# Expert blocks of a two-layer MoE kernel: 184 blocks in 46 groups become 176 blocks in 44 groups, in another order

## The chip, the cores and the metric

The kernel runs on one core of a Trainium2 chip, as one launch. The metric is the device time of that launch in microseconds (us); a kernel's time is the median of its runs. TensorE is called PE here (its matmuls; its weight loads are PEld), VectorE DVE, ScalarE ACT, GpSimd POOL, and SP is the engine whose queue issues most DMAs.

## The reference

Two layers over 2048 tokens of 1024 features. Layer 0 mixes the tokens with latent attention, layer 1 with pooled means; each is followed by a layer norm, a mixture of experts and a second layer norm. Both experts parts are alike:

```
g_sel  = argmax(h @ w_grp + b_grp)                 # one of 8 groups
top_p, top_i = top_k(softmax(e_logits of that group), 2)
expert = g_sel * 8 + top_i                         # 2 of 64 experts for each token
gate   = g_gate * top_p / sum(top_p)
y      = (silu(x @ w1[e]) * (x @ w3[e])) @ w2[e]   # d_expert = 256
out[token] += y * gate
```

So 4096 choices (2048 tokens, two each) are spread over 64 experts in each layer, unevenly, and every expert's 3 MB of weights (w1, w3 and w2, 1 MB each, float32) are needed once in each layer.

## The kernel before

The router (Router, lines 457 to 638) counts, token tile by token tile, how many tokens chose each expert. Once 14 of the 16 tiles are counted it sorts the experts by that count. An expert's position in this sort is its *place*: place 0 is the expert with the most tokens. Places 13 to 16 are an exception: they hold four experts of the middle, chosen after nine tiles, so that their weights can be fetched early. What a place means is fixed when the program is written; which expert stands at it is data.

Work is cut into blocks of 32 slots (QS). A block (p, q) holds the tokens number 32q to 32q+31 of the expert at place p. Four blocks make a group of 128 rows (function groups). Each place has a fixed number of blocks, by AT4, AT3 and AT2: 6 for places 0 to 2, 4 for places 3 to 12, 3 for places 13 to 36, and 2 for places 37 to 63. That is 184 blocks in 46 groups. Tokens that find no slot are done by overflow(), a loop whose number of turns is counted on the chip by counts(); it is entered with zero turns if every expert fits.

WORK is the order of the groups, and LINE the order in which their places come up first. Moe.main runs one step for each group in WORK. Step i gathers 128 token rows for step i+3 (an indirect DMA on POOL's queue), multiplies group i with w1 and w3 (up, line 1313: 64 matmuls that read up to four experts' weights), multiplies the group of step i-1 with w2 (down, line 1341: 32 matmuls) and scatters its rows to memory, then transposes the rows of a later group (line 1301) and the activations of group i (line 1326). PE executes this in program order.

load_line (line 1277) writes the weight loads into SP's queue in the order of LINE: for each place w13 (two DMAs of 1 MB, line 1249) and w2 (one, line 1254). There are five w13 and five w2 buffers in layer 0, six and six in layer 1; place number n of LINE reuses the buffer of number n-5 or n-6, once the last group that reads that one is done (ENDS). SP is in order: a load that waits for its buffer holds up those behind it. The first three places' weights (nine DMAs) are loaded before the experts begin. The DMA semaphores are eight that go round, so a load is issued when the eighth one before it has landed.

Behind layer 1's last group, ending() and rest() fetch what the last norm reads (w<-ln_g, w<-ln_b, ten w<-X, six fx<-X; lines 973, 974, 1608, 1616) into weight buffers that have come free. After overflow's loop last_norm reads Y.

Router.finish (line 625) makes the tables of source rows, target rows and gates for all groups, with one pair of small matmuls for each run that block_runs finds; counts() makes each place's limit lim (lines 1425, 1426).

Of the kernel before, what the change touches and what calls it, by code (L numbers as in the profile page):

```python
# [25 lines left out]
NE = 64  # L26
HP = P // 2
QS = 32
NQ = P // QS
RANKS = 192  # L30

AT4, AT3, AT2 = 3, 13, 37
NPRE = 4
FIRST_ORDER_AT = 8
ORDER_AT = 13
# [34 lines left out]
def groups():  # L70

    sixes = [[(p, q) for q in range(4)] for p in range(AT4)]
    fours = [[(p, q) for q in range(4)] for p in range(AT4, AT3)]
    rests = [[(p, 4), (p, 5), (AT2 + p, 0), (AT2 + p, 1)] for p in range(AT4)]
    line = [(p, q) for p in range(AT3, AT2) for q in range(3)]
    threes = [line[i:i + NQ] for i in range(0, len(line), NQ)]
    line = [(p, q) for p in range(AT2 + AT4, NE) for q in range(2)]
    twos = [line[i:i + NQ] for i in range(0, len(line), NQ)]
    every = sixes + fours + rests + threes + twos
    n = [0]  # L80
    for x in (sixes, fours, rests, threes, twos):
        n.append(n[-1] + len(x))
    big = [[g] for g in range(n[1], n[2])] + [[g, n[2] + g] for g in range(n[1])]
    mid = [[g, g + 1, g + 2] for g in range(n[3], n[4], 3)]
    small = [[g] for g in range(n[4], n[5])]
    work = mid.pop(0)
    for i in range(len(big)):
        for part in (small, big, mid if i % 3 == 1 else []):
            if part:
                work = work + part.pop(0)  # L90
    work += [g for part in (mid, small) for x in part for g in x]
    assert sorted(work) == list(range(len(every)))
    return every, work


GROUPS, WORK = groups()
G = len(GROUPS)

# [4 lines left out]
def block_runs():  # L103

    def steps(x):
        return slice(x[0], x[-1] + 1, x[1] - x[0] if len(x) > 1 else 1)

    found = {}
    for g, blocks in enumerate(GROUPS):
        for j, (p, q) in enumerate(blocks):  # L110
            kind = next(i for i, end in enumerate((AT3, AT2, AT2 + AT4, NE)) if p < end)
            found.setdefault((kind, j, q), []).append((p, g))
    out = []
    for (_, j, q), run in found.items():
        ps, gs = [p for p, _ in run], [g for _, g in run]
        for x in (ps, gs):
            assert len({b - a for a, b in zip(x, x[1:])}) <= 1, x
        out.append((j, q, steps(ps), steps(gs)))
    return out
# [347 lines left out]
class Router:  # L467
# [157 lines left out]
    def finish(self, pool, tag):  # L625
        nc, c, w = self.nc, self.c, self.work
        flat = w.tile([P, RANKS], F32, name="ohp", bufs=2)
        nc.vector.tensor_copy(flat, self.ptab)
        pf = self.psum.tile([P, 2, G], F32, name="plog")
        for j, q, places, gs in block_runs():  # L630
            nc.tensor.matmul(pf[j * QS:(j + 1) * QS, :, gs], flat[:, q * QS:(q + 1) * QS], self.perm[:, :, places],
                             start=True, stop=True, tile_position=(0, j * QS))
        val = w.tile([P, 2, G], F32, name="fval", bufs=1)
        nc.vector.tensor_copy(val, pf)
        self.isrc, self.idst = slot_rows(nc, w, pool, val[:, 0, :], G, tag)
        self.gate = pool.tile([P, G], F32, name=f"gate{tag}")
        nc.vector.tensor_copy(self.gate, val[:, 1, :])
# [582 lines left out]
class Moe:  # L1220
# [180 lines left out]
    def counts(self):  # L1401

        nc, c, r, pool = self.nc, self.c, self.r, self.pool

        def col(name, n=1):
            return pool.tile([NE, n], F32, name=name, bufs=1)

        pc = self.psum.tile([P, 2, F], F32, name="ph", bufs=2)
        nc.tensor.matmul(pc[:NE, 0, 0:1], r.ohsum, c.onesb[:, 0:1], start=True, stop=True)
        own = col("cown", 2)  # L1410
        nc.vector.tensor_copy(own[:, 0:1], pc[:NE, 0, 0:1])
        nc.vector.tensor_copy(own[:, 1:2], c.tok1[:NE, 0:1])
        yield

        pc = self.psum.tile([P, 2, F], F32, name="ph", bufs=2)
        nc.tensor.matmul(pc[:NE, 0, 0:2], r.perm[:NE, 0, :], own, start=True, stop=True)
        cnt = col("cnt", 2)
        nc.vector.tensor_copy(cnt, pc[:NE, 0, 0:2])
        yield

        lim = col("lim")
        nc.vector.memset(lim, -6.0 * QS)
        step = col("limstep")
        for start, n in ((AT4, 2), (AT3, 1), (AT2, 1)):
            nc.vector.tensor_scalar(step, c.tok1[:NE, 0:1], start + 0.5, float(n * QS), op0=ALU.is_gt, op1=ALU.mult)
            nc.vector.tensor_tensor(lim, lim, step, op=ALU.add)
        nc.vector.tensor_scalar(lim, lim, -1.0, None, op0=ALU.mult)
        thr = col("thr", S // P)
        nc.vector.tensor_scalar(thr, c.iota[:NE, 0:S // P], float(P), lim, op0=ALU.mult, op1=ALU.add)
        cmp = col("cmp", S // P)  # L1430
        nc.vector.tensor_scalar(cmp, thr, cnt[:, 0:1], None, op0=ALU.is_lt)
        ov = col("ov1")
        nc.vector.tensor_reduce(ov, cmp, axis=AX.X, op=ALU.add)
        pcum = self.psum.tile([P, 2, F], F32, name="ph", bufs=2)
        nc.tensor.matmul(pcum[:NE, 0, 0:1], c.triinc[:NE, :NE], ov, start=True, stop=True)
        yield
        cum = col("cum", 2)
        nc.vector.tensor_copy(cum[:, 1:2], pcum[:NE, 0, 0:1])
        nc.vector.tensor_tensor(cum[:, 0:1], cum[:, 1:2], ov, op=ALU.subtract)
        member, after = col("member", NE), col("after", NE)  # L1440
        nc.vector.tensor_scalar(member, c.iota[:NE, 0:NE], cum[:, 0:1], None, op0=ALU.is_ge)
        nc.vector.tensor_scalar(after, c.iota[:NE, 0:NE], cum[:, 1:2], None, op0=ALU.is_ge)
        nc.vector.tensor_tensor(member, member, after, op=ALU.subtract)
        yield
        first = col("first")
        nc.vector.tensor_scalar(first, cum[:, 0:1], float(-P), lim, op0=ALU.mult, op1=ALU.add)
        vals = col("vals", 2 * NE)
        nc.vector.tensor_scalar(vals[:, 0:NE], member, cnt[:, 1:2], None, op0=ALU.mult)
        nc.vector.tensor_scalar(after, member, float(FAR), float(-FAR), op0=ALU.mult, op1=ALU.add)
        nc.vector.tensor_scalar(vals[:, NE:], member, first, None, op0=ALU.mult)  # L1450
        yield
        pb = self.psum.tile([P, 2, F], F32, name="ph", bufs=2)
        nc.tensor.matmul(pb[:, 0, 0:2 * NE], c.ones[:NE, :], vals, start=True, stop=True)
        nc.tensor.matmul(pb[:, 0, 2 * NE:3 * NE], c.ones[:NE, :], member, start=True, stop=True)
        nc.tensor.matmul(pb[:, 0, 3 * NE:3 * NE + 1], c.ones[:NE, :], ov, start=True, stop=True)
        self.bl = pool.tile([P, 2, NE], F32, name="bl", bufs=1)
        bl = self.bl
        valid = pool.tile([P, NE], F32, name="valid", bufs=1)
        nc.vector.tensor_copy(valid, pb[:, 0, 2 * NE:3 * NE])
        nc.vector.tensor_tensor(bl[:, 0, :], pb[:, 0, 0:NE], valid, op=ALU.subtract)  # L1460

        nc.vector.tensor_scalar(bl[:, 1, :], valid, float(-FAR), float(FAR), op0=ALU.mult, op1=ALU.add)
        nc.vector.tensor_tensor(bl[:, 1, :], bl[:, 1, :], pb[:, 0, NE:2 * NE], op=ALU.add)
        nc.vector.scalar_tensor_tensor(bl[:, 1, :], c.iota[:, 0:NE], float(P), bl[:, 1, :], op0=ALU.mult, op1=ALU.add)
        self.total = pool.tile([1, 1], I32, name="total", bufs=1)
        nc.vector.tensor_copy(self.total, pb[0:1, 0, 3 * NE:3 * NE + 1])
        self.jt = pool.tile([P, 1], F32, name="jt", bufs=1)
        nc.vector.memset(self.jt, 0.0)
# [196 lines left out]
```

## Time and profile before

| | us |
|---|---|
| median of 3 runs | 3085.59 |
| the runs | 3077.85 to 3090.36 |
| the profiled execution | 3076.86 |
| its span | 3075.2 |
| layer 0's groups: first up to end of the last down | 1524.8 to 2111.9 |
| layer 1's groups: first up to end of the last down | 2402.8 to 2975.1 |

Times in the trace are counted from the span's start. The two stretches of experts are 1159 us of the 3075. In the rows below "w<-in_w_dram" is a weight load, "ph" the result of up, "py" of down, "xg<-X,isrc" the gather and "Y<-y,idst" the scatter. Such a row of the order of time gives start, duration, engine, line and operation, how many instructions were merged, and in brackets how long the engine had been idle before it and what ended that.

### The profile page before, as it was taken

Reading aid. Unit: us, or ns where it says so; the run is one execution under the profiler, and the core shown is the slowest. Engines: PE = TensorE matmul, PEld = TensorE weight load, DVE = VectorE, ACT = ScalarE, POOL = GpSimd, SP = SyncE. Lnnn points to the kernel's source line nnn. Section 1 sums busy time; section 2 is a strip of 40 time slices with the busy share of each in tenths; the row PEclk is TensorE's granted clock in tenths of the full one; section 3 lists DMA queues with packets and bytes.
Section 4 is the critical chain, followed back from the end, with each engine's and each line's share of the span. In section 5 each row is a group of like instructions: output and inputs, shape, how many; then the busy total and the mean of one; then the engine's idle time right before and its main releaser. Section 6 shows DMA issues by size and latency. Waiting matters only on the chain.

```text
span 3075.2 us, 50829 instructions
## 1 busy us (share of the span) xinstructions
PE 2697.8 (88%) x19378; PEld 1507.0 (49%) x19378; DVE 1516.2 (49%) x3756; ACT 864.3 (28%) x1465; POOL 972.0 (32%) x838
## 2 busy tenths in 40 slices
PE   6987888888888888999799999897888799999977
PEld 5864554445454454688533333333777333333323
DVE  7655677677676776445521111223998221111118
ACT  4444343334343334323211111112454111111102
POOL 4244455455454544321211111112542111111100
PEclk9997999999999999999899999998898899999988
DMA  6544122121221211545699999995424899999967
GB/s 209 184 147 157 46 70 70 56 77 53 70 66 50 77 32 50 156 150 186 235 368 418 412 415 399 374 418 208 176 92 193 320 419 417 415 410 411 416 264 293
DMA packets 230242, 690.22 MB, mean 224 GB/s; under 512 B 42318, under 2 KB 102990, under 8 KB 180588
## 3 DMA queue, kind: packets, MB, share of 16 engines
q1 hardware_dynamic: 191484, 586.01, 50.2%
q0 software_dynamic: 27104, 69.90, 5.9%
q10 hardware_dynamic: 11408, 31.02, 2.6%
q8 instruction: 155, 2.54, 0.3%
q14 instruction: 91, 0.75, 0.1%
HBM read 595.47 MB, written 120.71 MB: 233 GB/s over the span
## 4 chain that ended last, share of the span: by engine, by line
PE 30%; DMA 20%; DVE 6%; issue 2%; POOL 1%; SPq 0%; ACT 0%; DVEq 0%; POOLq 0%; ACTq 0%; another core or an unknown queue 0%
DMA w<-in_w_dram 16%; PE ph L1313 12%; PE py L1341 5%; PE pz L1050 5%; PE pt L1301 2%; PE plog L501 2%; PE fz L1529 1%; DVE ohp L568 1%; DMA pw<-in_pool_w_dram 1%; DMA xg<-X,isrc 1%; PE rpt L992 1%; DVE goh L512 0%; DMA fy<-Y 0%; PE pz L1193 0%; PE ptab L572 0%
## 5 line engine op out<-in xcount | busy, mean ns | idle before, releaser
L1313 PE MATMUL ph<-w,xT 128*32 128x512 f32 x5888 | 682.4, 603 | 38.9 <-DMA w<-in_w_dram 38.8
L1313 PEld LDWEIGHTS ph<-w,xT 128*32 128x32 f32 x5888 | 199.5, 111 | 448.8 <-issue 430.2
L879 POOL TENSOR_TENSOR acc<-acc,pe 128x512 f32<-128x512 f32 (+3 forms) x256 | 307.5, 1201 | 348.6 <-ACT pe L865 339.5
L865 ACT ACTIVATE pe<-sc 128x1024 f32<-128x1024 f32 (+1 forms) x320 | 280.8, 896 | 429.6 <-DVE sc L863 234.7
L1270 POOL DMA_INDIRECT Y<-y,idst x92 | 92.1, 1001 | 935.2 <-ACT xT L1302 873.1
L785 DVE TENSOR_REDUCE mx<-pm 128x2 f32<-128x1024 f32 (+2 forms) x320 | 339.9, 1062 | 84.2 <-PE pm L677 79.3
L1318 DVE SCALAR_TENSOR_TENSOR h<-sg,gate,ph 128x256 f32<-128x256 f32 x92 | 44.1, 480 | 657.1 <-ACT sg L1316 657.1
L1341 PE MATMUL py<-w,hT 128*32 128x512 f32 x2944 | 348.7, 592 | 1.6 <-DVE hT L1328 1.6
L677 PE MATMUL sc<-qn,k 64*128 64x512 f32 (+2 forms) x1920 | 272.8, 390 | 5.6 <-ACT rl L824 5.6
L677 PE MATMUL po<-pe,vt 128*64 128x512 f32 (+3 forms) x1280 | 270.7, 544 | 0.0
L677 PE MATMUL pm<-k,qn 64*128 64x512 f32 (+2 forms) x640 | 146.9, 452 | 116.1 <-DVE mx L785 109.4
L1316 ACT ACTIVATE sg<-ph 128x256 f32<-128x256 f32 x92 | 35.4, 384 | 725.8 <-PE ph L1313 713.8
L878 DVE TENSOR_TENSOR acc<-acc,pe 128x512 f32<-128x512 f32 (+3 forms) x256 | 216.2, 845 | 9.7 <-ACT pe L865 8.8
L677 PEld LDWEIGHTS sc<-qn,k 64*128 64x128 f32 x1920 | 181.8, 198 | 70.0 <-issue 26.3
L1341 PEld LDWEIGHTS py<-w,hT 128*32 128x32 f32 x2944 | 106.4, 110 | 214.2 <-issue 212.6
L677 PEld LDWEIGHTS pm<-k,qn 64*128 64x128 f32 x640 | 64.9, 194 | 234.1 <-DVE mx L785 140.0
L1343 DVE COPY y<-py 128x512 f32<-128x512 f32 x92 | 63.6, 692 | 224.4 <-PE py L1341 224.4
L677 PEld LDWEIGHTS po<-pe,vt 128*64 128x64 f32 x1280 | 78.5, 137 | 131.2 <-issue 123.3
L1301 PEld LDWEIGHTS pt<-ident,xg 128*128 128x128 f32 x736 | 90.3, 194 | 97.6 <-issue 72.9
L1301 PE MATMUL pt<-ident,xg 128*128 128x128 f32 x736 | 108.2, 291 | 23.5 <-DMA xg<-X,isrc 22.1
L677 PE MATMUL pm<-ka,qa 64*128 64x512 f32 (+2 forms) x640 | 125.1, 382 | 0.0
L677 PE MATMUL sc<-qb,kb 33*128 33x512 f32 (+2 forms) x640 | 124.5, 380 | 0.0
(361 smaller groups left out, 4317.6 us busy)
## 6 DMA issues: line engine op xcount, KB each, us to landing
w<-in_w_dram SPq DMA_DIRECT2D x384, 1024.0 KB
fy<-Y SPq DMA_DIRECT2D x16, 1024.0 KB
OT<-ot SPq DMA_DIRECT2D x31, 512.0 KB
K<-kq SPq DMA_DIRECT2D x32, 256.0 KB
V<-v SPq DMA_DIRECT2D x16, 512.0 KB
QN<-kq SPq DMA_DIRECT2D x32, 256.0 KB
qn<-QN SPq DMA_DIRECT2D x32, 256.0 KB
qb<-QR SPq DMA_DIRECT2D x128, 64.0 KB
```

Of the source, the lines that this page charges most:

```text
L501: nc.tensor.matmul(pl, xT(k), self.wr[:, k, :], start=(k == 0), stop=(k == ND - 1))
L677: return self.pin(self.nc.tensor.matmul(*a, **kw))
L785: self.pin(nc.vector.tensor_reduce(mx[:, :, tt, ch], pm[:, :, :n], axis=AX.X, op=ALU.max))
L865: nc.scalar.activation(pe[:, :, c0:], sc[:, :, c0:], AF.Exp, scale=SCALE)
L878: self.pin(self.nc.vector.tensor_tensor(acc[:, 0, c0:], before[:, 0, c0:], pe[:, 0, c0:], op=ALU.add))
L879: self.nc.gpsimd.tensor_tensor(acc[:, 1, c0:], before[:, 1, c0:], pe[:, 1, c0:], op=ALU.add)
L1050: nc.tensor.matmul(pz, o[:, a, k, :], wo.parts[k][b][:, hs], start=(n == 0), stop=(n == 3 * ND - 1))
L1270: st = self.nc.gpsimd.indirect_dma_start(out=self.Y, out_offset=bass.IndirectOffsetOnAxis(ap=idx, axis=0), in_=y, in_offset=None, bounds_c ...
L1301: self.pin(nc.tensor.transpose(pt[:, j, :], x[:, half * 4 + j, :], self.c.ident))
L1313: self.pin(nc.tensor.matmul(ph[js], xT[:, k, js], w[:, :, k, :], start=(k == 0), stop=(k == ND - 1), tile_position=(0, j * n)))
L1341: self.pin(nc.tensor.matmul(py[js], hT[:, k, js], w[:, k, hs], start=(k == 0), stop=(k == NF - 1), tile_position=(0, j * n)))
L1343: (nc.vector.tensor_copy if half else nc.scalar.copy)(y[:, hs], py)
```

## The change

Places 1 and 2 lose their sixth block (AT5 = 1: only place 0 keeps six), the places with three blocks end at 34 instead of 36, and the last four places (60 to 63) have one block instead of two. That is 176 blocks in 44 full groups. The two freed blocks in the groups of rests go to places 60 and 61, and the last two one-block places, 62 and 63, share the last group of the threes. The order changes too: the groups of the places with most blocks come first among the large ones instead of last, and small, large and middle groups alternate until all are used up. counts() follows the new limits with five steps instead of three.

```diff
--- before.py
+++ after.py
@@ -29,7 +29,7 @@
 NQ = P // QS
 RANKS = 192
 
-AT4, AT3, AT2 = 3, 13, 37
+AT5, AT4, AT3, AT2, AT1 = 1, 3, 13, 35, 60
 NPRE = 4
 FIRST_ORDER_AT = 8
 ORDER_AT = 13
@@ -71,25 +71,26 @@
 
     sixes = [[(p, q) for q in range(4)] for p in range(AT4)]
     fours = [[(p, q) for q in range(4)] for p in range(AT4, AT3)]
-    rests = [[(p, 4), (p, 5), (AT2 + p, 0), (AT2 + p, 1)] for p in range(AT4)]
-    line = [(p, q) for p in range(AT3, AT2) for q in range(3)]
+    rests = [[(p, 4), (0, 5) if p == 0 else (AT1 + p - 1, 0), (AT2 + p, 0), (AT2 + p, 1)] for p in range(AT4)]
+    line = [(p, q) for p in range(AT3, AT2) for q in range(3)] + [(p, 0) for p in range(AT1 + AT4 - 1, NE)]
     threes = [line[i:i + NQ] for i in range(0, len(line), NQ)]
-    line = [(p, q) for p in range(AT2 + AT4, NE) for q in range(2)]
+    line = [(p, q) for p in range(AT2 + AT4, AT1) for q in range(2)]
     twos = [line[i:i + NQ] for i in range(0, len(line), NQ)]
     every = sixes + fours + rests + threes + twos
     n = [0]
     for x in (sixes, fours, rests, threes, twos):
         n.append(n[-1] + len(x))
-    big = [[g] for g in range(n[1], n[2])] + [[g, n[2] + g] for g in range(n[1])]
-    mid = [[g, g + 1, g + 2] for g in range(n[3], n[4], 3)]
+    big = [[g, n[2] + g] for g in range(n[1])] + [[g] for g in range(n[1], n[2])]
+    mid = [list(range(g, min(g + 3, n[4]))) for g in range(n[3], n[4], 3)]
     small = [[g] for g in range(n[4], n[5])]
     work = mid.pop(0)
-    for i in range(len(big)):
+    i = 0
+    while big or mid or small:
         for part in (small, big, mid if i % 3 == 1 else []):
             if part:
                 work = work + part.pop(0)
-    work += [g for part in (mid, small) for x in part for g in x]
-    assert sorted(work) == list(range(len(every)))
+        i += 1
+    assert sorted(work) == list(range(len(every))) and all(len(x) == NQ for x in every)
     return every, work
 
 
@@ -108,7 +109,7 @@
     found = {}
     for g, blocks in enumerate(GROUPS):
         for j, (p, q) in enumerate(blocks):
-            kind = next(i for i, end in enumerate((AT3, AT2, AT2 + AT4, NE)) if p < end)
+            kind = next(i for i, end in enumerate((AT3, AT2, AT2 + AT4, AT1, AT1 + AT4 - 1, NE)) if p < end)
             found.setdefault((kind, j, q), []).append((p, g))
     out = []
     for (_, j, q), run in found.items():
@@ -1421,7 +1422,7 @@
         lim = col("lim")
         nc.vector.memset(lim, -6.0 * QS)
         step = col("limstep")
-        for start, n in ((AT4, 2), (AT3, 1), (AT2, 1)):
+        for start, n in ((AT5, 1), (AT4, 1), (AT3, 1), (AT2, 1), (AT1, 1)):
             nc.vector.tensor_scalar(step, c.tok1[:NE, 0:1], start + 0.5, float(n * QS), op0=ALU.is_gt, op1=ALU.mult)
             nc.vector.tensor_tensor(lim, lim, step, op=ALU.add)
         nc.vector.tensor_scalar(lim, lim, -1.0, None, op0=ALU.mult)
```

The engines' programs move with it. On PE, layer 1's last two steps before, with the numbered weight buffers that they read (w13 in up, w2 in down; pt2 is the transpose between them):

```order
L1313 MATMUL ph_26240<-w13_25798,xT_26143 32x512 x2
L1313 MATMUL ph_26240<-w13_25978,xT_26143 32x512 x2
...
L1326 MATMUL pt2_26301<-ident_73,h_26275 128x128 x2
L1313 MATMUL ph_26306<-w13_25978,xT_26222 32x512
L1313 MATMUL ph_26306<-w13_25984,xT_26222 32x512 x3
...
L1326 MATMUL pt2_26367<-ident_73,h_26341 128x128 x2
L1341 MATMUL py_26373<-w2_26072,hT_26370 32x512
L1341 MATMUL py_26373<-w2_26077,hT_26370 32x512 x3
```

And the last two steps of layer 1 now:

```order
L1314 MATMUL ph_25926<-w13_25560,xT_25819 32x512 x3
L1314 MATMUL ph_25926<-w13_25653,xT_25819 32x512
...
L1327 MATMUL pt2_25987<-ident_73,h_25961 128x128 x2
L1314 MATMUL ph_25992<-w13_25653,xT_25908 32x512 x2
L1314 MATMUL ph_25992<-w13_25746,xT_25908 32x512
L1314 MATMUL ph_25992<-w13_25752,xT_25908 32x512
...
L1327 MATMUL pt2_26053<-ident_73,h_26027 128x128 x2
L1342 MATMUL py_26059<-w2_25741,hT_26056 32x512 x2
L1342 MATMUL py_26059<-w2_25840,hT_26056 32x512
L1342 MATMUL py_26059<-w2_25845,hT_26056 32x512
```

Before, the last up reads one place for the first time; now it reads the last two of LINE for the first time, and the last down their w2.

On SP's queue, the end of layer 1's weight loads and the loads behind them before (in brackets the semaphores that the instruction waits for: DMAHW is one of the eight of the DMAs, PE the release of a buffer):

```order
L1249 DMA w_25978<-in_w_dram 128x2048 [waits DMAHW3_49,PE_49]
L1249 DMA w_25984<-in_w_dram 128x2048 [waits DMAHW5_49,PE_49]
L1249 DMA w_25984<-in_w_dram 128x2048 [waits DMAHW6_49]
L1254 DMA w_26072<-in_w_dram 128x2048 [waits DMAHW7_49,PE_49]
L1254 DMA w_26077<-in_w_dram 128x2048 [waits DMAHW0_49,PE_49]
L973 DMA w_26396<-in_ln_g_dram 128x1024 [waits DMAHW1_49,PE_49]
L974 DMA w_26396<-in_ln_b_dram 128x1024 [waits DMAHW2_49]
L1608 DMA w_26399<-X_61 128x1024 [waits DMAHW3_49]
...
L1608 DMA w_26409<-X_61 128x1024 [waits DMAHW3_49,PE_49]
...
L1616 DMA fx_26416<-X_61 128x1024 [waits DMAHW5_49,PE_49]
```

The same end now:

```order
L1250 DMA w_25746<-in_w_dram 128x2048 [waits DMAHW3_49]
L1250 DMA w_25752<-in_w_dram 128x2048 [waits DMAHW5_49]
L1250 DMA w_25752<-in_w_dram 128x2048 [waits DMAHW6_49]
L1255 DMA w_25840<-in_w_dram 128x2048 [waits DMAHW7_49,PE_49]
L1255 DMA w_25845<-in_w_dram 128x2048 [waits DMAHW0_49,PE_49]
L1609 DMA w_26085<-X_61 128x1024 [waits DMAHW1_49,PE_49]
...
L1609 DMA w_26090<-X_61 128x1024 [waits DMAHW5_49,PE_49]
L974 DMA w_26082<-in_ln_g_dram 128x1024 [waits DMAHW6_49,PE_49]
...
L1609 DMA w_26095<-X_61 128x1024 [waits DMAHW3_49,PE_49]
...
L1617 DMA fx_26102<-X_61 128x1024 [waits DMAHW5_49,PE_49]
```

The number of loads and their order at the end (two places' w13, then their two w2) are the same; the last w13 loads no longer wait for PE, and four of the w<-X loads have moved ahead of ln_g and ln_b.

## Rows read from the trace of the kernel before

**Rows 1.** The page: busy time by engine, and the DMAs in 40 slices.
```profile
PE 2697.8 (88%) x19378; PEld 1507.0 (49%) x19378; DVE 1516.2 (49%) x3756; ACT 864.3 (28%) x1465; POOL 972.0 (32%) x838
DMA  6544122121221211545699999995424899999967
GB/s 209 184 147 157 46 70 70 56 77 53 70 66 50 77 32 50 156 150 186 235 368 418 412 415 399 374 418 208 176 92 193 320 419 417 415 410 411 416 264 293
```
**Rows 2.** Order of time on PE, layer 1: one step without a wait.
```profile
2890.01 7.07 PE L1313 MATMUL ph<-w,xT 128*32 128x512 f32 x64
2896.90 3.62 PE L1341 MATMUL py<-w,hT 128*32 128x512 f32 x32
2900.45 1.16 PE L1301 MATMUL pt<-ident,xg 128*128 128x128 f32 x8
2901.44 0.40 PE L1326 MATMUL pt<-ident,h 128*128 128x128 f32 x2
2901.77 7.07 PE L1313 MATMUL ph<-w,xT 128*32 128x512 f32 x64
```
**Rows 3.** Windows: stretch, length, busy us by engine, PE clock, DMA share, GB/s.
```profile
1600.00:1700.00 100.00, 94.43 (x824) 36.62 (x816) 17.55 (x32) 12.46 (x24) 16.22 (x16) 0.99 1.02 418
2500.00:2600.00 100.00, 97.01 (x858) 36.70 (x854) 17.55 (x32) 12.45 (x24) 16.54 (x17) 0.98 1.02 418
2800.00:2900.00 100.00, 98.21 (x884) 35.93 (x876) 18.02 (x33) 13.43 (x26) 16.16 (x16) 1.00 1.01 412
```
**Rows 4.** The chain of waits in layer 1: start, duration, what.
```profile
2794.99 24.47 DMA w<-in_w_dram
2819.49 23.39 DMA w<-in_w_dram
2842.87 0.14 issue
2843.01 6.60 PE ph L1313 x57
```
**Rows 5.** SP's queue, end of layer 1: weight loads, then the last norm's.
```profile
2912.48 8.47 SPq L1249 DMA_DIRECT2D w<-in_w_dram  x4
2924.07 3.09 SPq L1254 DMA_DIRECT2D w<-in_w_dram  x2
2959.38 0.34 SPq L973 DMA_DIRECT2D w<-in_ln_g_dram  x1
```
**Rows 6.** Order of time, all engines: layer 1's last up, and fx.
```profile
2959.70 7.07 PE L1313 MATMUL ph<-w,xT 128*32 128x512 f32 x64
2975.16 3.90 SPq L1616 DMA_DIRECT2D fx<-X  x6
```
**Rows 7.** SP's queue and PE at the end of layer 0.
```profile
2069.18 0.86 SPq L1249 DMA_DIRECT2D w<-in_w_dram  x2
...
2062.07 7.08 PE L1313 MATMUL ph<-w,xT 128*32 128x512 f32 x64
...
2096.47 7.07 PE L1313 MATMUL ph<-w,xT 128*32 128x512 f32 x64
```
**Rows 8.** Windows: the end of layer 0, the start and the end of layer 1.
```profile
2060.00:2075.00 15.00, 15.00 (x136) 5.84 (x132) 3.90 (x7) 2.14 (x4) 1.88 (x2) 1.00 1.02 413
2075.00:2090.00 15.00, 15.00 (x142) 5.21 (x138) 2.19 (x4) 1.56 (x3) 1.09 (x2) 1.00 0.72 281
...
2411.00:2437.00 26.00, 25.34 (x230) 10.03 (x227) 5.55 (x14) 4.08 (x8) 4.02 (x4) 1.00 0.72 276
2437.00:2460.00 23.00, 23.00 (x214) 8.30 (x212) 5.52 (x17) 3.11 (x6) 4.05 (x4) 1.00 0.97 384
...
2920.00:2940.00 20.00, 20.00 (x184) 7.41 (x180) 4.38 (x8) 3.11 (x6) 1.99 (x2) 1.00 0.86 353
```
**Rows 9.** PE behind a wait, layer 1: a short one, a longer one.
```profile
2636.17 6.63 PE L1313 MATMUL ph<-w,xT 128*32 128x512 f32 x58 [1.84 <-DMA w<-in_w_dram]
...
2663.60 8.33 PE L1313 MATMUL ph<-w,xT 128*32 128x512 f32 x58 [2.85 <-DMA w<-in_w_dram]
```
**Rows 10.** The page: POOL's DMA queue (gathers and scatters).
```profile
q0 software_dynamic: 27104, 69.90, 5.9%
```
**Rows 11.** Groups of DVE, around layer 0's router tables.
```profile
L1426 DVE TENSOR_TENSOR lim<-lim,limstep 64x1 f32<-64x1 f32 x3 | 0.4, 146 | 0.0
```
**Rows 12.** The chain of waits: layer 0's first gather, and after layer 1.
```profile
1513.43 9.45 DMA xg<-X,isrc
...
2978.74 10.72 DMA fx<-X
```

## The prediction

> **What bounds the kernel now.** I read the page first, then the order of time on PE in the two stretches of experts, then the chain of waits, then SP's queue. On the page PE is 88% busy, and the slices hold two plateaus in which the DMAs move about 415 GB/s [rows 1]; these are the experts of the two layers. The diff touches nothing else but a few small instructions before them.
>
> A step that waits for nothing takes 11.76 us on PE: its up starts at 2890.01 and the next at 2901.77, and up, down and the two transposes stand in it end to end [rows 2]. 46 steps make 541 us, yet layer 1's ups run from 2402.8 to 2959.7. Its first up is at 0 steps and its last at 45, which is 529.2 us without waits, so 27.7 us are lost between. In the chain the loss has one name: weight loads. PE resumes at 2843.01 when a load issued at 2819.49 lands, 23.4 us after its issue, and the loads before it in the chain each follow on the landing of the one eight before [rows 4]. The queue is full there, and the windows say so too: 418, 418 and 412 GB/s at a DMA share of 1.01 to 1.02, while PE is 94 to 98% busy [rows 3]. Both are nearly saturated, so neither saving can be taken alone.
>
> How far PE is behind the loads at a layer's end is the number that matters. In layer 1 the last w13 DMA is the fourth of those that begin at 2912.48 and end at 2912.48 + 8.47 = 2920.95, each issue 0.33 long, so it is issued at 2920.6 [rows 5]. With the 23.4 us of the queue it lands at 2944.0. The last up starts at 2959.70 [rows 6]: 15.7 us later. Before that PE runs ten steps without a wait, on work that it had put off. In layer 0 the last w13 is not issued until 2069.18, because its buffer comes free when the up that begins at 2062.07 ends (7 us later); the last up there starts at 2096.47 [rows 7].
>
> **The change, part by part.** *Two groups less in each layer.* Removed on PE: 2 x 11.76 = 23.5 us in each layer, 47.0 in all, with their gathers, scatters, copies and activations, which lie beside PE. This is the gain if PE alone were the bound. But the 192 weight DMAs of a layer stay, and so do the rows that are gathered and scattered: 4096 choices fill fewer empty slots. POOL's queue moved 69.90 MB [rows 10], some 33 MB of it in each layer's experts (4096 rows of 4 KB, twice). Without the nine weight DMAs that are loaded ahead and three more that go out while the router ends, 180 MiB of weights and 33 MB of rows are 222 MB, which at 416 GB/s take 534 us; 44 steps take 517. So in the changed kernel the loads are later than PE by the end of a layer, and the last up waits for the last w13. What can be had is the distance by which PE trailed, not the 23.5.
>
> The Trainium skill has a rule that speaks for more: DMA: Bandwidth & Descriptors, section Where 436 GB/s comes from, puts the ceiling of the 16 DMA engines at 435 GB/s, but says that for transfers from HBM the HBM share of a core, about 358, binds. The second half does not agree with this trace (412 to 418 GB/s over 100 us, rows 3); at 435, an estimate by that page, the 222 MB would take 511 us and PE would be the bound again. No window of 100 us in a layer shows a rate above 418.
>
> *Layer 1.* The number of loads before the last w13 and their order at the end are unchanged, so it lands where it did, 2944.0, moved by what the new order does to the stream earlier. A load waits for its buffer. The first six reuses wait for the same groups as before. Then the loads of LINE's numbers 12, 14, 16 and 21 have to wait for a group one later (an 11.76 us step), number 18 for one earlier. Before, the stream lost 26 x (1 - 276/418) = 8.8 us in the window 2411 to 2437, and 23 x (1 - 384/418) = 1.9 us in 2437 to 2460 [rows 8]; the first loss stays, the second is of the kind that can come once or twice more. From below it is 0, from above 2 x 1.9 = 4; I take 2. After a wait of over 2 us the up runs 8.33 us instead of 6.63 [rows 9]: 1.7. The last up then starts at 2944.0 + 2 = 2946.0 instead of 2959.7, less 1.7: gain 12.0, range 6 to 16. Both last w2, issued 3.5 and 6.2 us after that w13, land before the last down needs them (8.7 + 3.4 + 1.3 us after the last up's start).
>
> *The last norm's loads.* They now wait for later groups in relation to the end. Before, ln_g went out at 2959.38, 0.3 us before the last up began [rows 5, 6], and fx at PE's end, landing 14.3 us after 2975.16 (2978.74 + 10.72) [rows 6, 12]. Now four of the ten w<-X are freed earlier, by the up before the last, but the rest only by the end of the last up and the down behind it (7.0 to 10.4 us after its start). 9 MiB in all; 2 are done early, so 7 MiB from there on at 416 GB/s are 17.6 us, from 7 to 10 us after the last up's start: done at 25 to 28, where before it was 29.8. Against that stands that fx still waits for PE's end and for its 10.7 us behind the rest. I take 0, bounds 3 us of gain and 6 of loss (the six MiB before fx in one piece).
>
> *Layer 0.* Its last w13 waited for a buffer, and that wait goes: number 63 of LINE now reuses a buffer that is free three steps before the last. What is late next is the stream itself. It carried 413 GB/s to 2075 and 281 in the next 15 us [rows 8], where it waited for buffers; without that it would have ended at 2075 + 15 x 281/413 = 2085.2, and the last w13, with two w2 loads behind it at 2.95 each (23.4/8), at 2079.3. That is by bytes. In layer 1 the bytes run dry at 2920 + 20 x 353/416 = 2937 [rows 8], so its last w13 is there at 2931 by bytes and lands at 2944, 13 us later. So 2079 to 2092; I take the middle, 2085, and again 2 for the shift and 1.7 for the slower up. Gain 2096.5 - 2088.7 = 7.8, range 2 to 14. The loads for the pool mixer begin at step 30 as before and cost what they cost.
>
> *Small parts.* counts() gets four more DVE instructions of 146 ns [rows 11] before the tables, finish() three more pairs of matmuls: 0.5 us in each layer, in front of the first gather and so on the path. 1.0 us.
>
> **Sum.** 12.0 + 0 + 7.8 - 1.0 = 18.8 us. The profiled execution was 3076.86 us (its span 3075.2), which gives 3058. It is faster than all three runs that were timed (3077.85 to 3090.36, median 3085.59), so a median lies above it, by 9 us in these; I add 5, halfway: before 3082, and the forecast 3063.
>
> **The rivals.** *PE stays the bound.* Both layers shorten by 23.5: 3082 - 47 + 1 = 3036. It needs the last w13 8 us sooner in layer 1 (2936) and 12 in layer 0 (2073). For it: PE is busier than anything in the last ten steps. Against it: the windows at 412 to 418 [rows 3], and that every wait before those ten steps is for a load. 6%.
>
> *The stream moves later and eats the distance.* Twice the shifts that I took and the landing at the late end: 4 instead of 2 in each layer, 2092 in layer 0, 6 us of loss in the tail. Gains 10 + 0 - 6 - 1 = 3 us: 3079. For it: the new order brings the places that hold two buffers for a long time to the front, where the queue fills. 18%.
>
> *Slower: the buffers starve the stream.* If the loads held back by one step (numbers 12, 14, 16 and 21) each leave the queue empty as in 2411 to 2437, a layer loses 8.8 us for each. It turns the sign from the second time in each layer on, since 2 x 8.8 = 17.6 is more than the 15.7 and the 11.5 (2096.5 - 2085) that there are to be had. Three times in both layers: 52.8 lost against 27.2, and the slower ups and small parts 4.4: 30 us slower, 3112. Against it: eight loads are in the queue, which is 23.4 us of work, two steps' worth. 6%.
>
> *It does not do what it says.* A block less could send tokens into the overflow loop. Counted with the reference's router on its inputs, no place overflows: in layer 0 place 60 has 29 choices for 32 slots, in layer 1 exactly 32 for 32. One token routed otherwise in layer 1 would cost a turn of the loop: the gather 9.45 [rows 12], three loads in a full-length pass (12 us for a place's three at the rate above and their latency), an up and a down, and 32 rounds of one-hot on DVE and PE: an estimate of 50 us, 3113. 2%.
>
> **How the numbers follow.** The forecast gets 68%, with a range of its own of 3055 to 3073: gains of 9 to 27, where the two layers together run from 8 to 30 and not all ends fall on one side. About 0.5% of the time, 15.4 us, is what a measurement of this kernel can tell from no change. Of the forecast's 68, some 45 lie above that gain and 23 below. Faster: 45 + 6 = 51%. Within 0.5%: 23 + 18 = 41%. Slower: 8%. The range takes in the second rival with a few us for the median's own scatter and, from below, half of the way from the forecast's range to the first: 3046 to 3083.
>
> **What would show it.** Right: 88 scatters and 44 steps in each layer; the last up of both layers waits for a weight load; the DMA plateau runs to the end of each stretch with no gap before ln_g; the last w13 of layer 1 is issued within 4 us of where it was, counted from layer 1's first up (517.8 us after it before); the waits of PE for weights grow from the 27.7 us that layer 1 loses to about 37. Wrong: ups that follow each other at 11.76 to the end (PE is the bound), windows of 280 GB/s in the first 150 us of a layer (starved buffers), or a last w13 that is issued over 15 us later than before.

## The result, and the profile after

| | before | after |
|---|---|---|
| median of the runs, us | 3084.18 (7 runs, 3077.85 to 3090.36) | 3063.21 (7 runs, 3052.78 to 3069.55) |
| ratio, 95% interval | | 0.9931 [0.9912, 0.9949] |
| the profiled execution (its span) | 3076.86 (3075.2) | 3052.78 (3050.8) |

The changed kernel is 21 us faster, 0.69%; a median of 3063 had been forecast, with a gain of 18.8. The two profiled executions are 24.1 us apart. Cut at landmarks of the trace:

| us | before | after | less | forecast |
|---|---|---|---|---|
| span's start to layer 0's first up | 1524.8 | 1517.5 | 7.3 | 0 |
| layer 0, first up to last up | 571.7 | 561.9 | 9.8 | 7.8 |
| layer 0's last up to layer 1's first up | 306.3 | 306.2 | 0.1 | -1.0 in all |
| layer 1, first up to last up | 556.9 | 543.7 | 13.3 | 12.0 |
| layer 1's last up to the first load of Y (fy) | 30.4 | 34.5 | -4.1 | 0 |
| from there to the end | 85.1 | 87.2 | -2.1 | 0 |

The three rows of the experts that were forecast give 19.0 us, against 19.8 (18.8 with the small parts). (An up is placed by its start. The -1.0 stands for both layers' small parts; layer 0's half of it falls into the first row.) The 7.3 us of the first row cannot be put down to the change: up to there the programs differ by the small parts alone, and over all kernels of this study the first up of layer 0 came anywhere from 1517.5 to 1536.9. Lengths inside a layer repeat much better: two later kernels whose layer 0 is that of before and of after had 571.6 and 561.5 (e10 and e9, below). So a layer's rows can be read to about a microsecond, and the total only by many runs.

The page of the changed kernel, the rows that answer to [rows 1] and [rows 10], and the group of the scatters (line numbers after are one higher):

```profile
PE 2661.6 (87%) x18966; PEld 1494.4 (49%) x18966; DVE 1507.8 (49%) x3748; ACT 858.4 (28%) x1453; POOL 964.4 (32%) x830
GB/s 210 186 148 158 46 71 57 67 71 63 64 74 50 78 29 54 143 157 177 239 357 418 410 414 416 369 415 250 179 93 187 319 418 415 418 415 413 407 313 280
q0 software_dynamic: 25952, 69.90, 6.0%
L1271 POOL DMA_INDIRECT Y<-y,idst x88 | 87.9, 998 | 922.2 <-ACT xT L1303 849.1
```

There are 88 scatters, and POOL's queue moves 69.90 MB, as before: the slots that went were empty, and to drop them saved no bytes. The slices have the two plateaus of [rows 1], a little shorter. PE's busy time fell by 36.2 us, not by the 47 of four steps: by the order of time the rest of an up behind a wait ran 1.3 to 2.5 us longer than it does otherwise eleven times in the changed kernel and six times before, which makes some 10 of the 11 us. Windows of the changed kernel, for [rows 3] and [rows 8]: stretch, length, busy us by engine, clock, DMA share, GB/s.

```profile
1600.00:1700.00 100.00, 95.35 (x824) 37.05 (x827) 16.97 (x31) 11.75 (x23) 16.18 (x16) 0.98 1.01 418
...
2394.00:2420.00 26.00, 25.34 (x229) 10.03 (x228) 6.01 (x14) 3.83 (x9) 4.01 (x4) 1.00 0.70 266
2420.00:2443.00 23.00, 23.00 (x211) 7.90 (x209) 5.06 (x17) 3.07 (x6) 4.04 (x4) 1.00 1.00 395
...
2780.00:2880.00 100.00, 94.97 (x818) 35.68 (x813) 15.84 (x29) 11.28 (x22) 14.10 (x14) 0.98 1.01 409
2903.00:2923.00 20.00, 20.00 (x184) 7.35 (x180) 3.91 (x7) 2.73 (x5) 1.96 (x2) 1.00 0.86 350
2923.00:2943.00 20.00, 19.17 (x176) 6.02 (x172) 3.01 (x6) 2.02 (x5) 1.95 (x2) 1.00 0.59 214
```

The transfers carry what they did, 409 to 418 GB/s; PE in layer 1's late window is 95% busy where it was 98. The early stretch, 8 to 58 us behind the first up, has 266 and 395 GB/s where before it had 276 and 384, and the windows behind it have 419 and 417 (2443 to 2483, 2483 to 2583): the new order starves the stream no more than the old one. Now the chain of waits at the end of layer 1 (start, duration, what), which answers to [rows 4]:

```profile
2808.34 24.49 DMA w<-in_w_dram
...
2832.84 24.85 DMA w<-in_w_dram
...
2857.82 8.29 PE ph L1314 x57
...
2929.24 7.00 PE ph L1314 x64
2936.24 3.50 PE py L1342 x32
...
2941.53 10.34 DMA w<-X
...
2951.88 11.13 DMA fx<-X
...
2963.62 4.93 DMA fy<-Y
```

PE is released by a load for the last time at 2857.82 (the up of the seventh step from the end), and from there to the last up nothing on the chain is a wait. Before, the last release was at 2843.01, ten steps ahead of the end. SP's queue at that end, for [rows 5]:

```profile
2896.70 9.02 SPq L1250 DMA_DIRECT2D w<-in_w_dram  x4
2908.00 2.82 SPq L1255 DMA_DIRECT2D w<-in_w_dram  x2
2925.41 11.18 SPq L1609 DMA_DIRECT2D w<-X  x5
2939.72 0.34 SPq L974 DMA_DIRECT2D w<-in_ln_g_dram  x1
...
2940.59 4.94 SPq L1609 DMA_DIRECT2D w<-X  x5
2945.63 6.57 SPq L1617 DMA_DIRECT2D fx<-X  x6
```

The last w13 is the fourth of the first row: issued at 2905.4, 519.9 us after layer 1's first up at 2385.5 (517.8 before). The trace records the semaphore updates of each load, and the last of this load's came at 2927.4: that is when it landed. The forecast's 23.4 us of a full queue would have made it 2928.8. The last up begins at 2929.2. Stream and PE arrive within two microseconds of each other.

### The profile page after: what moved, and what is told of

It reads as the page before. It is cut to its first block, busy times and chain, and to the rows that moved or that the text cites. A ratio compares the mean times of both kernels' runs of the same rounds, so it can differ in the third digit from the quotient of the medians.

```text
span 3050.8 us, 49943 instructions
## 1 busy us (share of the span) xinstructions
PE 2661.6 (87%) x18966; PEld 1494.4 (49%) x18966; DVE 1507.8 (49%) x3748; ACT 858.4 (28%) x1453; POOL 964.4 (32%) x830
## 3 DMA queue, kind: packets, MB, share of 16 engines
q0 software_dynamic: 25952, 69.90, 6.0%
## 4 chain that ended last, share of the span: by engine, by line
PE 27%; DMA 22%; DVE 7%; issue 2%; POOL 1%; SPq 0%; ACT 0%; DVEq 0%; POOLq 0%; ACTq 0%
DMA w<-in_w_dram 19%; PE ph L1314 10%; PE pz L1051 5%; PE py L1342 5%; PE pt L1302 2%; PE plog L502 1%; PE fz L1530 1%; DVE ohp L569 1%; DMA pw<-in_pool_w_dram 1%; DMA xg<-X,isrc 1%; PE rpt L993 1%; PE pz L1194 1%; DVE ov L571 1%; PE ptab L573 0%; DMA fy<-Y 0%
## 5 line engine op out<-in xcount | busy, mean ns | idle before, releaser
L1314 PE MATMUL ph<-w,xT 128*32 128x512 f32 x5632 | 668.3, 611 | 49.3 <-DMA w<-in_w_dram 49.1
L1342 PE MATMUL py<-w,hT 128*32 128x512 f32 x2816 | 337.2, 592 | 1.7 <-DVE hT L1329 1.7
L1317 ACT ACTIVATE sg<-ph 128x256 f32<-128x256 f32 x88 | 33.8, 384 | 722.4 <-PE ph L1314 710.2
L678 PE MATMUL sc<-qa,ka 64*128 64x512 f32 (+2 forms) x640 | 123.8, 378 | 0.0
```

The source lines that it names most:

```text
L678: return self.pin(self.nc.tensor.matmul(*a, **kw))
L1314: self.pin(nc.tensor.matmul(ph[js], xT[:, k, js], w[:, :, k, :], start=(k == 0), stop=(k == ND - 1), tile_position=(0, j * n)))
L1342: self.pin(nc.tensor.matmul(py[js], hT[:, k, js], w[:, k, hs], start=(k == 0), stop=(k == NF - 1), tile_position=(0, j * n)))
```

## The experiments

Two theories stood against each other at the start. *A*: the four groups less make the gain, cut short because the weight stream becomes the bound. *B*: the new order makes it, by moving buffers and waits. Lengths below are from a layer's first up to the start of its last up and, behind the stroke, to the end of its last down; "fy" is from layer 1's first up to the first load of Y. A star marks a last up that begins on the weights that are there and then waits for the others: its start comes early, and there only the second length can be compared.

| | median, us | ratio to before | layer 0 | layer 1 | fy |
|---|---|---|---|---|---|
| before | 3084.18 | | 571.7 / 587.0 | 556.9 / 572.3 | 587.3 |
| after | 3063.21 | 0.9931 [0.9912, 0.9949] | 561.9 / 577.3 | 543.7 / 559.1 | 578.1 |
| e1 new blocks, old order | 3063.53 | 0.9934 [0.9911, 0.9958] | 554.0* / 572.2 | 536.7* / 561.1 | 573.3 |
| e2 old blocks, new order | 3077.73 | 0.9976 [0.9961, 0.9991] | 566.9 / 582.3 | 552.6 / 568.0 | 583.2 |
| e3 before, fewer loads | 3022.18 | 0.9788 [0.9765, 0.9811] | 537.7 / 553.1 | 528.9 / 544.3 | 555.8 |
| e4 after, fewer loads | 3013.19 | 0.9761 [0.9739, 0.9784] | 514.1 / 529.5 | 505.7 / 521.2 and one up more | 568.2 |
| e5 before, half an up | 3043.26 | 0.9858 [0.9835, 0.9881] | 554.9 / 566.9 | 534.2 / 546.1 | 564.8 |
| e6 after, half an up | 3063.62 | 0.9926 [0.9905, 0.9946] | 545.6* / 564.2 | 530.9* / 545.1 and one up more | 589.8 |
| e7 after, mixer's loads early | 3066.80 | 0.9936 [0.9913, 0.9959] | 555.0 / 570.4 | 543.4 / 558.8 | 577.9 |
| e8 e1, mixer's loads early | 3059.00 | 0.9916 [0.9899, 0.9933] | 552.7 / 568.1 | 537.9* / 562.4 | 574.7 |
| e9 after, fewer loads in layer 1 | 3027.88 | 0.9810 [0.9791, 0.9829] | 561.5 / 576.9 | 505.1 / 520.5 | 533.7 |
| e10 before, fewer loads in layer 1 | 3057.46 | 0.9913 [0.9896, 0.9931] | 571.6 / 586.9 | 528.9 / 544.3 | 554.9 |

Each ratio is to runs of the kernel before that were made together with that row's.

**Blocks or order (e1, e2).** e1 is the changed kernel with the old rule of order; e2 is the kernel before with the new one.

```diff
--- after.py
+++ e1
-    big = [[g, n[2] + g] for g in range(n[1])] + [[g] for g in range(n[1], n[2])]
+    big = [[g] for g in range(n[1], n[2])] + [[g, n[2] + g] for g in range(n[1])]
...
-    while big or mid or small:
+    for i in range(len(big)):
...
-        i += 1
+    work += [g for part in (mid, small) for x in part for g in x]
```

> 176 blocks in 44 groups as in the changed kernel, but the groups in the order rule of before (places with four blocks first, places 0 to 2 last, then what is left). Theory (the weight loads set each layer's end, and two steps less let PE follow them more closely): nearly the whole gain stays, 3060 to 3068 us against 3084 of before; the last steps wait for loads. Rival (the gain is the new order's, since buffers come free sooner at the end): about 3080 to 3086.

> 184 blocks in 46 groups as before, in the new order rule. Theory: 46 steps of 11.76 us stay, PE trails the loads at both ends as before, so 3076 to 3086 us; last ups that follow each other at 11.76 us. Rival (the order gives the gain): 3060 to 3068.

The blocks alone give 0.9934, the whole of the gain; the order alone gives 0.9976, some 7 us, and on top of the blocks nothing that shows in the medians. (To the end of the last down, e1 is 5.1 us shorter than the changed kernel in layer 0 and 2.0 longer in layer 1.) e1 also shows the end of layer 1 as the prediction had drawn it. PE there:

```profile
2931.49 1.06 PE L1313 MATMUL ph<-w,xT 128*32 128x512 f32 x6
2938.67 8.48 PE L1313 MATMUL ph<-w,xT 128*32 128x512 f32 x57 [6.12 <-DMA w<-in_w_dram]
```

and the last pieces of its chain before that up:

```profile
2895.54 21.64 DMA w<-in_w_dram
2917.20 21.34 DMA w<-in_w_dram
```

The last w13 is issued at 2917.20, 522.4 us after the first up, and lands 21.3 us later; the last up, begun on the weights that are there, waits 6.1 us for it. (So the 536.7 of the table counts an up that is not complete until 552.8.)

**Take the stream away (e3, e4).** Only the first five or six places' w2 are loaded, and the later places read those.

```diff
-                self.down_w[p] = self.load_down(...)
+                self.down_w[p] = self.load_down(...) if nd < self.ndown else self.down_w[LINE[nd % self.ndown]]
```

> Before, with w2 loaded only for the first five (layer 0) or six (layer 1) places; the later places multiply with these, so 59 and 58 of a layer's 192 weight DMAs are left out and the output is not the reference's. Theory (loads are what PE waits for): the waits of 42.5 and 27.7 us go, steps follow each other at 11.76 us, about 3015 us. Rival (PE's waits are for something else): over 3050.

> The changed kernel with the same loads left out as in e3. Theory: without a full stream PE alone sets the pace, and the two groups that each layer has less are worth 2 x 11.76 us each: 42 to 47 us below e3, about 2970 us. Rival (two groups are worth about 21 us whatever the loads do): 19 to 24 us below e3.

e3's total, 3022, lies 7 us above the 3015 that had been expected: layer 0 is still 8.5 us longer than its 45 steps from first up to last (529.2), as layer 0 of e4 is 8.4 us longer than its 43 (505.7). From the one kernel to the other the theory holds to the step in each layer: 537.7 less 514.1 is 23.6 and 528.9 less 505.7 is 23.2, where two steps of 11.76 are 23.5. The total of e4 does not follow it: 3013 instead of 2970. PE's order of time in e4 behind layer 1's last down has the reason:

```profile
2880.53 3.64 PE L1342 MATMUL py<-w,hT 128*32 128x512 f32 x32 [0.83 <-DVE hT L1329]
2887.28 15.28 PE L1485 MATMUL pt<-vs,ohv 128*128 128x2 f32 x64 [3.11 <-DVE ohv L1484]
...
2908.90 8.40 PE L1314 MATMUL ph<-w,xT 128*128 128x512 f32 x16
...
2919.36 3.70 PE L1342 MATMUL py<-w,hT 128*128 128x512 f32 x8 [0.52 <-DVE hT L1329]
```

This is a turn of the overflow loop: 64 matmuls of the search for the tokens, a gather, an up in full-length rows, a down, from 2884.2 to 2923.1. The altered output of layer 0 routes layer 1's tokens otherwise; the place that has exactly 32 tokens for its 32 slots is the likely one to get more, but no run shows which place it is. The turn takes PE 38.9 us; the last norm's loads run beside it, so the first load of Y is 33.9 us later for it (62.5 us behind the 44th up, 28.6 in e9 below, which has no such turn). Without it e4 would stand near 2979, an estimate, 43 us under e3.

**Take half of PE's up away (e5, e6).** Four of the eight k in each up, so the products are not the reference's.

```diff
-        for k in range(ND):
+        for k in range(ND // 2):
...
-... stop=(k == ND - 1), ...
+... stop=(k == ND // 2 - 1), ...
```

> Before, with half of the up matmuls left out (contraction over 4 of 8 pieces; the output is not the reference's), all loads kept: a step is 3.5 us shorter on PE. Theory (the stream of loads sets the layers' length): the layers end with the last weights, 3040 to 3058 us, only 26 to 44 us below before. Rival (PE sets it): 92 steps by 3.5 us, some 320 us less, 2765.

> The changed kernel with the same half of up left out as in e5. Theory: 46 or 44 groups make no difference when PE is far faster than the loads: within 6 us of e5. Rival (the groups' own gathers, scatters and copies cost something beside PE): 15 us or more below e5.

3.5 us less in each of 92 ups before are 322 us of PE's work; 41 came of it. With these loads the two kernels are nearly alike in both layers. By the start of the last up layer 0 seems to be 9.3 us shorter in e6 (554.9 and 545.6), but e5 finds the weights of its last up there, and e6 begins it and then waits. First e5, then e6:

```profile
2087.47 3.64 PE L1313 MATMUL ph<-w,xT 128*32 128x512 f32 x32
```
```profile
2078.58 1.06 PE L1314 MATMUL ph<-w,xT 128*32 128x512 f32 x6
2083.55 4.86 PE L1314 MATMUL ph<-w,xT 128*32 128x512 f32 x25 [3.91 <-DMA w<-in_w_dram]
```

To the end of the last down layer 0 takes 566.9 and 564.2 us, 2.7 apart, and layer 1 546.1 and 545.1, 1.0 apart. e6 has the overflow turn as well (an up 43.1 us behind the 44th); from its 44 groups' last down to the first load of Y it takes 44.8 us where e5 takes 18.7, so without the turn its total would be some 26 lower, near 3038 by estimate: 6 us under e5, the edge of what had been expected. A window of 100 us in layer 1 of e5, then of e6:

```profile
2500.00:2600.00 100.00, 81.65 (x605) 29.91 (x601) 17.56 (x32) 12.44 (x24) 16.06 (x16) 0.88 1.01 419
```
```profile
2500.00:2600.00 100.00, 70.63 (x538) 26.63 (x534) 15.96 (x30) 10.87 (x21) 16.07 (x16) 0.86 1.01 418
```

The DMA share is 1.01 with PE 71 to 82% busy: this is what a stream looks like that binds nearly alone. Even the stream ends sooner so: the last weight load of layer 1 landed 536.6 us after the first up in e5, by the trace's semaphore records, where it landed at 545.0 before and at 547.2 after. A PE that is behind holds buffers that loads wait for, which is the likely reason; no run separates it from others.

**The same in layer 1 only (e9, e10).** The condition of e3 and e4, for layer 1 alone; its routing stays the reference's.

> The changed kernel, but in layer 1 alone only the first six places' w2 are loaded and the others read these, so 58 MB less are streamed and layer 1's values are not the reference's; its routing is, since it comes before. Theory (without the loads only PE's 44 steps bind, and the overflow turn that was seen with fewer loads in both layers came from layer 0's altered output): 44 ups and no more, first up to last 43 x 11.76 = 506 us against 543.7, the total 3018 to 3028. Rival (the changed layer 1 has its turn of the overflow loop anyway): a 45th up 40 us later, total 3058 to 3068.

> The kernel before with the same fewer loads in layer 1 alone. Theory: 45 steps at 11.76 from first up to last, 529 us, against 556.9; layer 0 as before, 572. Total 28 us plus some 3 us in the tail under the kernel before: 3052 to 3058. The kernel after with fewer loads in layer 1 then lies 28 to 35 us lower: 23.5 in layer 1, the rest in layer 0. Rival (the two groups are hidden anyway and only the stream's order counts): the two lie within 15 us of each other.

e9 has 44 ups in layer 1 and no more, so the extra turn in e4 came with the altered routing. The two kernels lie 29.6 us apart: 23.7 in layer 1 and 10.0 in layer 0 by the traces, which leaves a loss of some 4 elsewhere. With the loads in place layer 1 gives 13.3 of its 23.7; the stream keeps the rest. PE in e9, one 100 us window, and in e10:

```profile
2800.00:2900.00 100.00, 100.00 (x906) 36.30 (x902) 19.43 (x36) 14.01 (x27) 14.43 (x15) 1.00 0.68 258
```
```profile
2800.00:2900.00 100.00, 100.00 (x908) 35.58 (x904) 18.03 (x33) 12.81 (x25) 16.54 (x17) 1.00 0.75 285
```

PE 100% busy with the DMA share at 0.68 to 0.75: here PE binds alone. The real kernels stand between these two pictures.

**A better version (e7, e8).** The pool mixer's weights are loaded in layer 0 beside the experts' weights, from step 30 on. One of these loads stands on the chain of the changed kernel, behind it the experts' loads that it held up:

```profile
1913.90 20.13 DMA pw<-in_pool_w_dram
...
1940.60 23.57 DMA w<-in_w_dram
1964.19 23.12 DMA w<-in_w_dram
1987.33 19.85 DMA w<-in_w_dram
...
2007.32 8.99 PE ph L1314 x57
```

e7 is the changed kernel, e8 is e1, both with

```diff
-MIX_AT = 30
+MIX_AT = 1
```

> The changed kernel with the pool mixer's building begun at step 1 of layer 0 instead of step 30 (MIX_AT). Theory: in layer 0 the mixer's loads (20.1 us in the chain for pool_w in the changed kernel, and its other loads behind it) hold up a stream of weights that is full at step 30 but not full in the first two steps; moved there they cost less, layer 0 ends 8 to 15 us sooner, 3048 to 3056 us. Rival (the loads cost the same wherever they stand, or the early weights come later): 3060 to 3070, with layer 0's waits moved from steps 30 to 37 to the first ten.

> The new blocks in the old order (the blocks alone gave 3063.5), with the pool mixer's loads begun at step 1 instead of 30. Theory (layer 0 is set by its weight stream, and the mixer's loads, 20 us in a full queue, hold it up late in the layer): layer 0 shortens from 554.0 us, first up to last, to some 547 as in the changed kernel with early loads (561.9 to 555.0), layer 1 stays at 537 and the total is 3054 to 3060. Rival (what the mixer's loads take is taken wherever they stand, and what is gained in layer 0 comes back between the layers): 3061 to 3067.

e7 missed: 3066.8. Its layer 0 is 6.9 us shorter in the trace, but the total is that of the changed kernel; the stretch from layer 0's last down to layer 1's first up was 6.6 us longer in its profiled execution. Over all kernels that stretch took 290.7 to 297.3 us, and the changed kernel and e7 are its two ends, so whether the gain is given back there is open. e8's total, 3059.0, is inside the range of its theory, but only in part by its step: to the end of the last down, layer 0 is 4.1 us shorter than e1's (568.1 and 572.2), where 7 had been expected. It is the fastest median of the kernels whose output is the reference's, yet its interval overlaps that of the changed kernel. It is no proven gain over it.

## Why the prediction was right, point by point

**The stream cuts the gain short**: shown. PE's steps alone would give 23.5 us in a layer (e3, e4, e9, e10 measure 23.2 to 23.7), and with the loads in place the layers gave 9.8 and 13.3. With half of PE's up gone layer 1's last up still ends 537.8 us (e5) and 536.8 us (e6) behind the first; the forecast had put the bytes of a layer at 534. By this the first rival, PE stays the bound at 3036, fell.

**The signs.** Of the signs that the prediction named, the 88 scatters, the issue of the last w13 and the growth of PE's waits came; a last up that waits for its weights did not, in either layer, nor did a plateau without a gap. The last six ups of each layer even follow each other without a wait, which it had named as the sign of PE as the bound; the waits before them, and e3, e4, e9 and e10, say that PE is not the only one.

**Layer 1, 12.0**: measured 13.3. The last w13 was to move by 2 us and its issue moved by 2.1 (517.8 to 519.9). PE's lost time grew from 27.7 to 38.0 (543.7 less 43 steps of 11.76); about 37 had been said. Wrong was the picture at the very end: the last up was to wait for its weights and then run 1.7 us longer. It does not wait. The semaphore records of the two traces tell when the last w13 landed (differences are taken before rounding):

| us from the layer's first up | last w13 landed | last up begins | PE behind |
|---|---|---|---|
| layer 0, before | 562.4 | 571.7 | 9.3 |
| layer 0, after | 560.0 | 561.9 | 1.8 |
| layer 1, before | 538.9 | 556.9 | 18.1 |
| layer 1, after | 541.9 | 543.7 | 1.8 |

So PE caught up 16.3 us and the load came 3.0 later. The prediction had PE 15.7 behind, because it gave the last load 23.4 us where it took 21.0; it had the load 2 later, no distance left and a slower up of 1.7, where the runs have 18.1, 3.0, a distance of 1.8 left and no slower up at the end. That these misses nearly cancel is luck. With the old order (e1) the same blocks do end in the wait, with 21.3 us from issue to landing.

The 1.7 of a slower up goes with the granted clock and not with the wait alone. The up behind the longer wait of [rows 9] stood in a window of 0.83 (2663 to 2673); in e1 an up of layer 0 ran its rest in 6.60 us behind a wait of 3.34, in a window of 1.00 (2070 to 2078). First the two windows, then that up:

```profile
2663.00:2673.00 10.00, 9.40 (x72) 3.32 (x76) 0.19 (x1) 0.39 (x1) 0.00 (x0) 0.83 1.01 415
```
```profile
2070.00:2078.00 8.00, 7.27 (x68) 2.69 (x72) 0.00 (x0) 0.21 (x1) 0.00 (x0) 1.00 1.00 416
```
```profile
2070.73 6.60 PE L1313 MATMUL ph<-w,xT 128*32 128x512 f32 x57 [3.34 <-DMA w<-in_w_dram]
```

**Layer 0, 7.8**: measured 9.8, in a range of 2 to 14. The wait of the last w13 for a buffer is gone: it is issued 540.2 us after the first up, where before it was 544.9. But it landed only 2.3 us sooner, at 560.0, where 562.2 had been forecast; the other 7.5 us of the gain are PE's distance, 9.3 us before and 1.8 after. Again no load is waited for at the end; PE in the changed kernel, for [rows 7]:

```profile
2068.48 7.07 PE L1314 MATMUL ph<-w,xT 128*32 128x512 f32 x64
...
2079.36 7.07 PE L1314 MATMUL ph<-w,xT 128*32 128x512 f32 x64
```

PE's last release by a load is at 2007.32, six ups ahead of the last. The middle of a wide range was taken, and it lay 2 us off; that is no more than a lucky choice. As in layer 1 the gain needs a PE that is behind: with half of its up gone (e5, e6) layer 0 shortens by 2.7 us, not by 9.8.

**The last norm's loads, 0**: measured a loss of 4.1, inside the bounds (3 of gain to 6 of loss). The step that failed: seven MiB were to run at 416 GB/s from 7 to 10 us behind the last up's start and be done after 25 to 28 us. They ran at 214 in the window from 2923 to 2943, since SP, in order, held ten w<-X and the two ln loads back at one release after another, and fx went out behind them at 2945.63 and landed at 2963.0, 33.8 us after the last up's start (29.8 before). So the plateau that was to run without a gap up to ln_g has one, 350 and then 214 GB/s. In e1 Y is read 12.3 us after the last down, in the changed kernel 19.0 us, before 14.9, in e2 15.2. No version tried the tail by itself: that this order of issues costs the 4 us is read from the trace, not shown.

**Small parts, 1.0**: not to be seen. The stretch that holds layer 1's share was 306.3 and is 306.2, and it scatters by more than that over the kernels (305.2 to 315.6).

**The other rivals.** Later stream (3079): the last w13 of layer 1 landed 3.0 us later, between the 2 of the forecast and the 4 of this rival, and that of layer 0 landed 2.3 sooner. Starved buffers (3112): the early windows are as they were. The overflow loop is not entered by the changed kernel (44 ups in each layer), but e4 shows how near it is, and a turn takes PE 38.9 us where 50 had been estimated. That 32 slots suffice is a matter of these inputs.

**The allowance of 5 us** for the median over the profiled execution: before, the seven runs' median lies 7.3 above it; after, 10.4. That the forecast's 3063 was met to a fraction of a microsecond is luck: before stands at 3084.2 and not at 3082, and the medians' gain is 21.0 and not 18.8, and these two cancel.

## What to carry to other kernels

Where PE and the transfers are both near full, ask for each how long it would take alone, and expect from a cut in one of them not much more than the distance by which it trails the other: here PE trailed by 9.3 and 18.1 us, and of the 23.5 us of work in each layer 9.8 and 13.3 came. Two kernels, one with less to load and one with less to multiply, measure both limits directly. A last wait that vanishes is no sign that its resource stopped binding: it may have been paid some steps earlier. And compare lengths up to the end of work, not to the start of it: a last up that begins early and then waits made 9.3 us out of 2.7 here.

## What the runs showed of the hardware beside that

With half of each up gone, PE's granted clock in the windows of e5 and e6 above was 0.86 to 0.88, against 0.98 to 1.00 in those of the changed kernel, e9 and e10; so e5 and e6 are not a PE at half its time. A mean of 0.86 to 0.88 lies between the two levels of 1.2 and 2.4 GHz, so part of the window ran at the lower one. One pw load for the mixer, which no expert reads, took 20.1 us on the chain of layer 0, about what a load of expert weights takes; with the mixer's loads moved to the first steps (e7) layer 0 is 6.9 us shorter.
